# Cosine-similarity attention on one core: three of 384 score tiles exponentiated off ScalarE, and new instruction orders

## The chip, the core and the metric

The kernel runs on one core of a Trainium2 chip. The metric is device time in microseconds (us); the kernel before takes 191.36 us, the median of five runs (191.32 to 191.49). Five engines work side by side, each through its own instruction queue in order: TensorE (PE; its weight loads are shown as PEld), VectorE (DVE), ScalarE (ACT), GpSimd (POOL) and SyncE (SP, which issues DMAs). [...]

## What is computed

Q, K and V have the shape 8 x 12 x 512 x 64 in float32, and tau is 0.1. Cut to what matters, the reference is:

```python
Q_norm = Q / (np.linalg.norm(Q, axis=-1, keepdims=True) + 1e-10)
K_norm = K / (np.linalg.norm(K, axis=-1, keepdims=True) + 1e-10)
scores = np.einsum('bhqd,bhkd->bhqk', Q_norm, K_norm) / tau
weights = np.exp(scores - np.max(scores, axis=-1, keepdims=True))
weights = weights / (np.sum(weights, axis=-1, keepdims=True) + 1e-10)
return np.einsum('bhqk,bhkd->bhqd', weights, V)
```

Since a cosine lies between -1 and 1, the scores lie between -10 and 10, and the kernel takes no maximum off.

## The kernel before

The 96 heads are worked in 48 pairs, s = 0 to 47. For each pair:

- LD and LV are the loads of Q, K (`LD.s.0`, `LD.s.1`) and V; ST is the store of the output. SP issues nearly all of them, in one list.
- SQ squares Q and K (POOL, line 229). SSQ sums groups of squares with eight matmuls (line 246) and RED ends the sum (DVE, line 253; for a few pairs RED alone, line 238). NEW is a chain of eight small DVE steps for two pairs at once, an inverse square root by bit pattern and Newton steps (lines 372 to 381).
- SCL multiplies Q (DVE) and K (POOL, line 270) by the inverse norms. TR transposes them on TensorE into the PSUM bank `x_ps` (line 277; seven pairs transpose K by a DMA, XT), and EVA copies that bank to SBUF (DVE, line 468).
- SCO makes scores: `SCO.s.c` is two matmuls of 128 keys by 512 queries, one for each head of the pair (line 481), into one half of the four-bank PSUM tensor `sc_ps`. `EXP.s.c` is one ScalarE instruction that exponentiates both tiles, 128 x 1024 elements, into the bfloat16 buffer `et` (line 498). Four of these make a pair. The two halves of `sc_ps` are used in turn, so SCO waits for the EXP before the last. In the last pair, c = 0 and 1 are head 0 and c = 2 and 3 are head 1, so that a head ends early, and `EXP.47.3` is cut in two (lines 490 to 495).
- VC casts V to bfloat16 (POOL, line 503). PV multiplies the weights by V and by a column of ones that gives the row sums: `PV.s.h.t`, four matmuls each (line 514), into `o_ps`. RCP and NRM divide by the sums (DVE, lines 526 to 530). The next pair's first PV waits for NRM, which frees `o_ps`. `final` (line 535) does this for the last pair in three pieces and other banks (lines 538 to 564).

The bank `x_ps` goes round in the order in which its users stand in TensorE's list: a user that carries `take="x"` waits until the previous one's reader, named in `until`, is done. `et` has three buffers, `qk` eighteen, `qt` five, `ob` eight.

The order of work on each engine is written out in `ORDER` (line 591), one list of names per engine, made beforehand by a planner. Each engine runs its list as it stands: an instruction that waits holds up all that is behind it. `WARM` and `FILL` (lines 587 and 588) are dummy matmuls at the start (line 216): 19 before anything else and 7 placed between the first transposes.

Of the kernel before, what the change touches and what calls it, by code (L numbers as in the profile page):

```python
# [3 lines left out]
ALU = mybir.AluOpType  # L4
ACT = mybir.ActivationFunctionType
# [118 lines left out]
def bass_cosine_similarity_attention_kernel(  # L124
# [7 lines left out]
    inv_tau = 1.0 / float(tau)  # L132
# [66 lines left out]
    def scores_read(s, c):  # L199

        if s < 0:
            return None
        return ("EXP", 0, 1, c - 2) if s == 0 else ("EXP", s, c)

# [196 lines left out]
    def pair(s):  # L401
# [73 lines left out]
        for c in range(NT) if s else ():  # L475
            b = c % 2

            def sco(e, c=c, b=b):
                for i in range(2):
                    h, k = (c // 2, 2 * b + i) if last_pair else (i, c)  # L480
                    last = e.matmul(  # L481
                        out=sc_ps[:, 2 * b + i, :], lhsT=qt[iqt][64 * h : 64 * h + 64, 1, k, :],
                        rhs=qt[iqt][64 * h : 64 * h + 64, 0, :, :], start=True, stop=True)
                return last

            P.add(("SCO", s, c), "pe",
                  [("SCO", s, c - 1) if c else None, *([("EVA", s, 0), ("EVA", 1, 1, c // 2) if s == 1 else ("EVA", 2, 1)] if s in (1, 2) else [("EVA", s)]), key("XT", s),
                   scores_read(s, c - 2) if c >= 2 else scores_read(s - 1, c + 2)], sco)
            before = [("SCO", s, c), scores_read(s, c - 1) if c else scores_read(s - 1, NT - 1), key("PV", s - R_ET, 1, NT - 1)]
            if last_pair:  # L490
                for i, (h, lo, hi) in enumerate(ENDS[1:] if c == NT - 1 else [(c // 2, 0, NT)]):
                    P.add(("EXP", s, c) + ((i,) if c == NT - 1 else ()), "act", before + [key("EXP", s, c, i - 1)],
                          lambda e, b=b, h=h, q=slice(128 * lo, 128 * hi): e.activation(
                              out=et[iet][:, 2 * b : 2 * b + 2, h, q], in_=sc_ps[:, 2 * b : 2 * b + 2, q],
                              func=ACT.Exp, scale=inv_tau))
            else:
                P.add(("EXP", s, c), "act", before,
                      lambda e, c=c, b=b: e.activation(  # L498
                          out=et[iet][:, c, :, :], in_=sc_ps[:, 2 * b : 2 * b + 2, :], func=ACT.Exp, scale=inv_tau))


# [8 lines left out]
        for h in range(2):  # L510
            for t in range(NT):
                def pv(e, h=h, t=t):
                    for c in range(NT):
# [8 lines left out]
                      [scores_read(s, NT - 1), ("VC", s), before, *([("EVA", 2, 1) if h else ("EVA", 1, 1, 1), ("EVA", 0, 1, 1)] if s == 0 else [])], pv,  # L522
# [11 lines left out]

    def final(s, iq, iet, io):


        bank = [n_ps[:, :, :].rearrange("p g x -> p (g x)"), x_ps[:, :], sc_ps[:, 0, :]]
        for i, (h, lo, hi) in enumerate(ENDS):
            for c in range(NT):  # L540
                def pv(e, i=i, h=h, c=c, lo=lo, hi=hi):
                    for t in range(lo, hi):
# [7 lines left out]
                      [("EXP", s, 3, i - 1) if i and c > 1 else ("EXP", s, 2 * h + c // 2), ("VC", s),  # L550
# [14 lines left out]

    for s in range(NP):
        pair(s)
# [6 lines left out]
    if FILL[1]:  # L574
# [13 lines left out]
FILL = (7, 0)  # L588
# [4 lines left out]
        LD.0.0.0 LD.0.0.1 LD.1.0 LD.2.1 LD.2.0 LD.3.1 LD.3.0 LD.4.0 LV.0 LD.4.1 LD.5.1 LD.5.0 LD.6.1 LD.6.0 LD.7.0  # L593
        LD.7.1 LV.1 LV.3 LD.11.0 LV.2 LD.9.1 LD.9.0 LD.8.1 LD.10.0 LV.7 LD.12.1 LD.8.0 LD.12.0 LV.4 LV.9 LV.5 LD.10.1
        LV.6 LD.13.0 LD.13.1 LD.22.1 LD.11.1 LV.10 LV.8 LD.25.1 LD.20.0 LD.15.1 LD.15.0 XT.9 ST.0 LD.14.1 LD.21.0
        LD.27.1 LD.14.0 ST.2 LV.11 LD.17.1 LD.18.0 LD.17.0 LD.28.1 LD.18.1 LD.16.1 ST.5 LD.16.0 ST.1 LV.14 LV.16 LV.13
        ST.3 LD.21.1 ST.4 LD.19.1 LV.12 LD.22.0 LV.15 LV.17 LD.19.0 XT.15 LD.24.0 LD.33.0 ST.6 ST.8 LV.18 LD.20.1 ST.7
        LD.23.0 LD.23.1 LD.29.1 LD.26.0 LV.22 LD.25.0 LD.26.1 ST.10 LV.19 LD.30.0 LV.23 ST.9 LD.36.1 LD.24.1 LD.28.0
        ST.15 LD.33.1 XT.21 LV.20 ST.13 LD.27.0 LV.21 ST.11 LV.25 ST.12 LD.31.1 ST.14 LV.26 LD.39.0 LD.29.0 LV.27
        LD.31.0 ST.19 LD.36.0 LV.24 LD.34.0 LV.28 LD.30.1 ST.17 LV.33 LD.34.1 ST.16 LD.32.0 ST.18 LD.32.1 XT.27 LV.29  # L600
        LV.30 ST.21 LD.41.0 LD.35.1 LV.31 ST.22 LD.37.0 LD.35.0 ST.20 ST.25 ST.24 LD.37.1 LD.38.0 LD.38.1 LD.40.1 LV.35
        LD.47.0 LD.40.0 LD.43.1 LD.42.1 XT.33 LV.32 LD.41.1 LV.36 ST.23 LD.39.1 LV.37 LD.44.1 LV.34 LD.45.0 ST.30
        LD.45.1 LD.44.0 ST.28 LV.39 LD.43.0 ST.26 LV.42 LD.47.1 LV.38 LD.42.0 LV.40 LV.43 ST.27 LD.46.0 LD.46.1 XT.39
        LV.45 ST.29 ST.32 ST.35 LV.41 ST.33 LV.44 ST.31 ST.36 ST.39 ST.34 LV.47 ST.40 ST.38 XT.45 ST.37 ST.41 LV.46
        ST.45 ST.43 ST.42 ST.44 ST.46 ST.47.0 ST.47.1""",
    "pool": """
        SQ.0.0.1 one eye vone SQ.2.1 SQ.2.0 SQ.3.0 VC.0 SQ.4.0 SQ.5.0 SQ.6.0 VC.1 SQ.7.0 SCL.4.1 VC.2 VC.3 SCL.5.1
        SQ.9.0 SQ.8.0 SCL.6.1 VC.4 VC.5 SCL.7.1 SQ.10.0 SCL.9.1 SCL.8.1 SQ.11.0 VC.6 SQ.13.0 VC.7 SQ.12.0 VC.9 SCL.10.1
        VC.8 SCL.11.1 SQ.15.0 SQ.14.0 VC.10 SCL.12.1 SQ.17.0 SQ.16.0 SCL.13.1 SCL.14.1 VC.11 SCL.15.1 SQ.21.0 SQ.18.0
        VC.12 VC.13 SQ.19.0 SCL.16.1 VC.15 VC.14 SCL.17.1 VC.16 VC.18 SQ.20.0 SCL.18.1 SCL.19.1 VC.17 SQ.22.0 SQ.23.0  # L610
        SCL.21.1 SCL.20.1 SQ.26.0 SQ.25.0 VC.19 SQ.24.0 SCL.22.1 VC.20 SCL.23.1 VC.21 SQ.28.0 SQ.27.0 SCL.24.1 SCL.25.1
        VC.22 SQ.29.0 VC.27 VC.23 SQ.31.0 SCL.26.1 VC.24 SCL.27.1 SQ.30.0 VC.26 SQ.34.0 SCL.28.1 VC.25 SQ.32.0 SCL.29.1
        SQ.33.0 SCL.31.1 SCL.30.1 SQ.35.0 VC.29 VC.28 SQ.36.0 SCL.33.1 SCL.32.1 SQ.38.0 VC.30 SQ.37.0 VC.31 SCL.34.1
        SQ.40.0 VC.32 SCL.35.1 VC.35 VC.33 SQ.39.0 SCL.37.1 VC.36 SCL.36.1 SQ.41.0 VC.37 VC.34 VC.39 SQ.45.0 SCL.38.1
        SCL.39.1 SQ.42.0 SQ.43.0 SCL.40.1 VC.42 VC.38 SCL.41.1 SQ.44.0 SQ.46.0 VC.44 VC.40 VC.41 VC.45 SCL.42.1 SCL.43.1
        SQ.47.0 SCL.45.1 VC.43 SCL.44.1 VC.47 SCL.46.1 VC.46 SCL.47.1""",
# [3 lines left out]
        NEW.0.0 NEW.0.1 EVA.2.0 NEW.0.2 EVA.2.1 NEW.0.3 NEW.0.4 NEW.0.5 RED.4.0 NEW.0.7 NEW.0.6 SCL.3.1 SCL.3.0 RED.5.0  # L620
        RCP.0 NEW.1.0 NRM.0 EVA.3 NEW.1.1 NEW.1.2 NEW.1.3 NEW.1.4 NEW.1.5 NEW.1.7 RED.6.0 NEW.1.6 SCL.4.0 RED.7.0 RCP.1
        NRM.1 EVA.4 NEW.2.0 NEW.2.1 NEW.2.2 SCL.5.0 NEW.2.3 RCP.2 NEW.2.4 NRM.2 EVA.5 NEW.2.5 NEW.2.6 SCL.6.0 NEW.2.7
        SCL.7.0 RED.9.0 RCP.3 NRM.3 RED.8.0 NEW.3.0 NEW.3.1 EVA.6 NEW.3.2 NEW.3.3 NEW.3.4 NEW.3.5 NEW.3.7 NEW.3.6 RCP.4
        NRM.4 EVA.7 SCL.9.0 RED.10.0 SCL.8.0 EVA.9 RCP.5 NRM.5 EVA.8 RED.11.0 RED.11.1 NEW.4.0 NEW.4.1 RCP.6 NEW.4.2
        NEW.4.3 RED.13.0 NRM.6 NEW.4.4 NEW.4.5 NEW.4.7 NEW.4.6 SCL.10.0 RED.12.0 NEW.5.0 SCL.11.0 NEW.5.1 EVA.10 NEW.5.2
        RCP.7 NEW.5.3 NRM.7 NEW.5.4 NEW.5.5 EVA.11 RED.15.0 NEW.5.6 NEW.5.7 SCL.12.0 RCP.8 NRM.8 RED.14.0 NEW.6.0
        NEW.6.1 SCL.13.0 NEW.6.2 NEW.6.3 NEW.6.4 EVA.12 RCP.9 NEW.6.5 NRM.9 NEW.6.7 RED.16.1 RED.17.0 NEW.6.6 RED.16.0
        SCL.14.0 EVA.13 NEW.7.0 NEW.7.1 RCP.10 NEW.7.2 NRM.10 EVA.14 NEW.7.3 NEW.7.4 SCL.15.0 RCP.11 EVA.15 NRM.11
        RED.21.0 NEW.7.5 RED.18.0 NEW.7.7 NEW.7.6 SCL.16.0 RCP.12 NRM.12 RED.19.0 NEW.8.0 NEW.8.1 NEW.8.2 SCL.17.0
        NEW.8.3 NEW.8.4 EVA.16 NEW.8.5 NEW.8.7 RCP.13 NRM.13 NEW.8.6 EVA.17 RED.21.1 SCL.19.0 SCL.18.0 RED.20.0 RCP.14  # L630
        NEW.9.0 NRM.14 EVA.18 NEW.9.1 NEW.9.2 EVA.19 NEW.9.3 NEW.9.4 RCP.15 NRM.15 NEW.9.5 NEW.9.7 RED.22.0 NEW.9.6
        SCL.20.0 RED.23.0 RCP.16 NEW.10.0 NRM.16 EVA.20 NEW.10.1 NEW.10.2 SCL.21.0 RCP.17 NEW.10.3 NRM.17 EVA.21
        NEW.10.4 NEW.10.5 RED.26.0 RED.26.1 NEW.10.7 RCP.18 NEW.10.6 NRM.18 RED.24.0 SCL.23.0 RED.25.0 SCL.22.0 NEW.11.0
        NEW.11.1 NEW.11.2 EVA.22 NEW.11.3 RCP.19 NRM.19 NEW.11.4 NEW.11.5 NEW.11.6 NEW.11.7 EVA.23 SCL.24.0 RCP.20
        NRM.20 RED.27.0 NEW.12.0 NEW.12.1 NEW.12.2 SCL.25.0 EVA.24 NEW.12.3 NEW.12.4 RCP.21 NRM.21 NEW.12.5 EVA.25
        NEW.12.6 NEW.12.7 RCP.22 NRM.22 SCL.26.0 RED.28.0 SCL.27.0 RED.29.0 NEW.13.0 NEW.13.1 NEW.13.2 NEW.13.3 NEW.13.4
        EVA.26 RCP.23 NEW.13.5 NRM.23 EVA.27 NEW.13.7 RED.31.1 NEW.13.6 SCL.28.0 RED.30.0 RED.31.0 RCP.24 NEW.14.0
        NRM.24 EVA.28 SCL.29.0 RCP.25 NRM.25 EVA.29 NEW.14.1 NEW.14.2 NEW.14.3 NEW.14.4 NEW.14.5 NEW.14.7 RED.32.0
# [124 lines left out]
```

## Time and profile before

| what | value |
|---|---|
| median of five runs | 191.36 us |
| the profiled execution's own time | 191.32 us |
| its span, first to last instruction | 189.5 us |
| time around the span | 1.82 us |
| busy: PE, DVE, ACT, POOL | 178.3, 150.4, 181.6, 160.3 us |
| EXP of 128 x 1024, 184 of them on line 498 | 168.9 us busy |
| granted TensorE clock | full |

The page is read like this. Busy time says how long an engine had work, not whether it set the end. The chain that ended last follows the work back from the last instruction to whatever released it at each step, so it names the engine on which a shorter instruction would be felt. A row of the costliest groups gives the source line, engine, operation, written and read tensors, shapes, count, busy time, the mean duration of one, and the idle time ahead of them. Since neighbours overlap, a group's busy time over its count is the pace, and the mean duration is longer.

### The profile page before, as it was taken

The page shows a single profiled execution, that of the slowest core. Times are in us where ns is not written, and L with a number is a line of the kernel's source. Part 1 is how long each engine was busy: PE and PEld are TensorE (multiplying, and loading weights), DVE is VectorE, ACT ScalarE, POOL GpSimd, SP SyncE. Part 2 cuts the span into 40 slices and gives each one's busy share as a digit, 9 for nine tenths or more (in the row PEclk, how much of TensorE's full clock was granted, in tenths as well). Part 3 has the DMA queues.
Part 4 walks back from the last instruction along what each step waited for, and adds up shares of the span by engine and source line. Part 5 has one row for each costly group of instructions (what it writes and reads, how often), then busy time and mean ns, then how long its engine had stood idle before and what let it go on. Part 6 is the DMA issues. An engine that isn't in the chain of part 4 may idle for free.

```text
span 189.5 us, 6453 instructions
## 1 busy us (share of the span) xinstructions
PE 178.3 (94%) x2622; PEld 114.0 (60%) x2622; DVE 150.4 (79%) x453; ACT 181.6 (96%) x208; POOL 160.3 (85%) x147
## 2 busy tenths in 40 slices
PE   7999999989998999999999999999999999998982
PEld 5546666656655666656665666656665666665641
DVE  2889998797987798788977978789798696886633
ACT  5799999999999999999999999999999999999992
POOL 1899899999999999999999979989999998555000
PEclk9999999999999999999999999999999999999999
DMA  6999999999999999999999999899999980393055
GB/s 191 352 350 351 348 350 314 283 363 332 319 270 273 367 345 313 296 278 378 303 309 276 289 302 293 257 275 324 290 281 277 273 258 11 116 225 135 3 167 171
DMA packets 56238, 51.68 MB, mean 273 GB/s; under 512 B 6928, under 2 KB 56208, under 8 KB 56208
## 3 DMA queue, kind: packets, MB, share of 16 engines
q1 hardware_dynamic: 55520, 50.67, 88.8%
q10 hardware_dynamic: 688, 0.59, 1.0%
q8 instruction: 21, 0.34, 0.9%
q14 instruction: 9, 0.07, 0.1%
HBM read 37.75 MB, written 12.58 MB: 266 GB/s over the span
## 4 chain that ended last, share of the span: by engine, by line
ACT 87%; PE 10%; DVE 1%; issue 0%
ACT et L498 86%; PE scps L216 3%; PE scps L481 2%; ACT et L351 2%; PE ops L514 1%; PE xps L246 1%; PE scps L346 1%; DVE ob L558 1%; PE xps L277 0%; PE nps L543 0%; PE ops L246 0%; PE ops L312 0%; PE xps L312 0%; DVE rd L556 0%; PE ops L277 0%
## 5 line engine op out<-in xcount | busy, mean ns | idle before, releaser
L498 ACT ACTIVATE et<-scps 128x1024 bf16<-128x1024 f32 x184 | 168.9, 1182 | 0.3 <-PE scps L481 0.3
L229 POOL TENSOR_TENSOR sq<-qk 128x1024 bf16<-128x1024 f32 (+2 forms) x48 | 87.8, 1843 | 4.5 <-DMA qk<-in_Q_dram 4.0
L481 PE MATMUL scps<-qt 64*128 64x512 bf16 x376 | 73.8, 386 | 5.8 <-ACT et L498 3.7
L514 PEld LDWEIGHTS ops<-vb,et 128*128 128x128 bf16 x1504 | 53.9, 98 | 25.6 <-issue 16.7
L514 PE MATMUL ops<-vb,et 128*128 128x65 bf16 x1504 | 68.5, 194 | 0.3 <-ACT et L498 0.2
L270 POOL TENSOR_TENSOR qn<-qk,rk 128x512 bf16<-128x512 f32 x44 | 45.9, 1054 | 8.3 <-DVE rk L377 7.3
L270 DVE TENSOR_TENSOR qn<-qk,nps 128x512 bf16<-128x512 f32 x49 | 33.0, 679 | 0.6 <-ACT nps L263 0.3
L528 DVE TENSOR_TENSOR ob<-ops,rd 128x512 f32<-128x512 f32 x47 | 32.4, 690 | 0.9
L481 PEld LDWEIGHTS scps<-qt 64*128 64x128 bf16 x376 | 18.4, 93 | 23.4 <-ACT et L498 8.4
L468 DVE COPY qt<-xps 128x1024 bf16<-128x1024 bf16 (+1 forms) x45 | 29.0, 644 | 3.8 <-PE xps L277 3.5
L503 POOL TENSOR_SCALAR vb<-vf 128x512 bf16<-128x512 f32 x48 | 29.9, 637 | 1.1 <-DMA vf<-in_V_dram 1.0
L277 PE MATMUL xps<-ident,qn 128*128 128x128 bf16 x340 | 27.1, 220 | 0.2
L277 PEld LDWEIGHTS xps<-ident,qn 128*128 128x128 bf16 x340 | 19.1, 98 | 10.3 <-DVE rd L526 4.1
L246 PE MATMUL xps<-sq,ident 128*128 128x128 bf16 x304 | 23.5, 220 | 0.2
L526 DVE RECIPROCAL rd<-ops 128x8 f32<-128x8 f32 x47 | 9.7, 206 | 15.7 <-PE ops L514 14.7
L246 PEld LDWEIGHTS xps<-sq,ident 128*128 128x128 bf16 x304 | 17.2, 98 | 7.0 <-issue 3.8
L253 DVE TENSOR_REDUCE nps<-xps 128x16 f32<-128x128 f32 x37 | 11.0, 297 | 6.5 <-PE xps L246 6.2
L238 DVE TENSOR_REDUCE nps<-sq 128x8 f32<-128x512 bf16 x16 | 10.8, 684 | 0.6 <-POOL sq L229 0.6
L372 DVE TENSOR_TENSOR nps<-nps,ys 128x32 f32<-128x32 f32 (+1 forms) x46 | 9.0, 195 | 1.0
L373 DVE SCALAR_TENSOR_TENSOR nps<-nps,ys 128x32 f32<-128x32 f32 (+1 forms) x46 | 8.8, 192 | 0.8
L216 PE MATMUL scps<-warm_in 128*128 128x256 bf16 x26 | 5.6, 402 | 1.1 <-DVE warm_in L214 1.1
L216 PEld LDWEIGHTS scps<-warm_in 128*128 128x128 bf16 x26 | 3.5, 143 | 2.5 <-DVE warm_in L214 1.1
(52 smaller groups left out, 51.9 us busy)
## 6 DMA issues: line engine op xcount, KB each, us to landing
vf<-in_V_dram SPq DMA_DIRECT2D x48, 256.0 KB, 4.7
qk<-in_Q_dram SPq DMA_DIRECT2D x47, 256.0 KB, 5.0
out_dram<-ob SPq DMA_DIRECT2D x47, 256.0 KB, 4.5
qk<-in_K_dram SPq DMA_DIRECT2D x46, 256.0 KB, 4.8
qk<-in_K_dram ACTq DMA_DIRECT2D x2, 256.0 KB, 3.6
qk<-in_Q_dram SPq DMA_DIRECT2D x2, 128.0 KB, 2.7
out_dram<-ob SPq DMA_DIRECT2D x1, 128.0 KB, 2.8
qt<-qn SPq DMA_TRANSPOSE x7, 4.3
```

Source lines behind the costliest of these rows:

```text
L216: P.add(key, "pe", needs, lambda e: e.matmul(out=bank[:, 0:256], lhsT=warm_in[:, 0:128], rhs=warm_in[:, :], start=True, stop=True))
L229: emit = lambda e: e.tensor_tensor(out=b, in0=a, in1=a, op=ALU.mult)
L246: last = e.matmul(out=ps[:, 0:128], lhsT=ident[:, :], rhs=sq[s % R_SQ][:, :, 8 * k : 8 * k + 8], start=(k == 0), stop=(k == 7))
L253: lambda e: e.tensor_reduce(out=dst(None), in_=ps[:, 0:128].rearrange("p (w g e) -> p w g e", w=2, e=8), axis=AX.X, op=ALU.add))
L270: lambda e: e.tensor_tensor(out=qn[iqn][:, w].rearrange("p t h d -> p h t d"), in0=qk[iq][:, w].rearrange("p h (t d) -> p h t d", t=NT), i ...
L277: last = e.transpose(dst[:, i, :], qn[s % R_QN][:, b // NT, b % NT].rearrange("p h d -> p (h d)"), ident[:, :])
L468: lambda e: e.tensor_copy(out=qt[iqt][:, :].rearrange("p w t x -> p (w t) x")[:, 0:nb], in_=tb[:, 0:nb]))
L481: last = e.matmul(out=sc_ps[:, 2 * b + i, :], lhsT=qt[iqt][64 * h : 64 * h + 64, 1, k, :], rhs=qt[iqt][64 * h : 64 * h + 64, 0, :, :], sta ...
L498: lambda e, c=c, b=b: e.activation(out=et[iet][:, c, :, :], in_=sc_ps[:, 2 * b : 2 * b + 2, :], func=ACT.Exp, scale=inv_tau))
L503: lambda e: e.tensor_scalar(out=vb[:, iq, :, :, 0:DIM].rearrange("p c h d -> p h c d"), in0=vf[iv][:, :, :].rearrange("p h (c d) -> p h c ...
L514: last = e.matmul(out=o_ps[:, h, 65 * t : 65 * t + 65], lhsT=et[iet][:, c, h, 128 * t : 128 * t + 128], rhs=vb[:, iq, c, h, :], start=(c = ...
L528: lambda e: e.tensor_tensor(out=ob[io][:, :], in0=grid[:, :, :, 0:DIM], in1=rd[io][:, :].unsqueeze(3).to_broadcast([128, 2, NT, DIM]), op= ...
```

## The change

The first two key tiles of work that leave ScalarE are the two tiles of `SCO.46.3`, and the third is the first tile of `SCO.47.0`. `OFFS` says where each is exponentiated. Each goes through `polynomial`: one matmul `SCOX` writes the scores into the bank `x_ps`; step 0 (DVE) multiplies and adds so that the result, converted to an integer, has the float's exponent in its upper bits; step 1 (DVE) keeps the mantissa bits; five Horner steps (2 to 6) evaluate a fifth-degree polynomial of the mantissa, the last one multiplying by the float made of the bits. On VectorE a Horner step is one `scalar_tensor_tensor` that keeps its running value in `x_ps` itself; on GpSimd it is a `tensor_scalar` and a `tensor_tensor` in SBUF. Scratch is taken from `qk` buffers that are no longer loaded.

`EXP.46.3` is gone, `EXP.47.0` covers one tile, and the halves of `sc_ps` are counted by the order of the EXPs that are left (`turn`). `FILL` goes from 7 to 4. All five lists of `ORDER` are written anew; ScalarE's differs in `EXP.46.3` and in the table load, which stands before `LD.1.1` instead of after it.

```diff
-    def scores_read(s, c):
-
-        if s < 0:
-            return None
+    live = [(s, c) for s in range(NP) for c in range(NT) if None in OFFS.get((s, c), (None,))]
+    turn = {sc: i for i, sc in enumerate(live)}
+
+    def scores_read(s, c, back=0):
+
+        s, c = live[turn[s, c] - back]
         return ("EXP", 0, 1, c - 2) if s == 0 else ("EXP", s, c)
...
-        for c in range(NT) if s else ():
-            b = c % 2
...
+        chunks = [c for c in range(NT) if (s, c) in turn]
+        for c in chunks if s else ():
+            b = turn[s, c] % 2
+            kept = [i for i in range(2) if i not in off(s, c)]
...
             P.add(("PV", s, h, t), "pe",
-                  [scores_read(s, NT - 1), ("VC", s), before, *([("EVA", 2, 1) if h else ("EVA", 1, 1, 1), ("EVA", 0, 1, 1)] if s == 0 else [])], pv,
+                  [scores_read(s, chunks[-1]), *(("OFF", s, c, i, 6) for c in range(NT) for i in off(s, c)), ("VC", s), before, *([("EVA", 2, 1) if h else ("EVA", 1, 1, 1), ("EVA", 0, 1, 1)] if s == 0 else [])], pv,
                   take=None if before else "o", until=("NRM", s))
...
+    def polynomial(s, c, i):
...
+        P.add(("SCOX", s, c, i), "pe", [("EVA", s), key("XT", s)], lambda e: e.matmul(
+            out=x_ps[:, :], lhsT=qt[iqt][hs, 1, k, :], rhs=qt[iqt][hs, 0, :, :], start=True, stop=True),
+            take="x", until=(*o, 6 if inside else 0))
+        gone = [n for p in (old, more) for n in (("SQ", p, 0), ("SCL", p, 0), ("SCL", p, 1))]
+        P.add((*o, 0), "dve", [("SCOX", s, c, i)] + gone, lambda e: e.tensor_scalar(
+            out=bits.bitcast(i32), in0=x_ps[:, :], scalar1=inv_tau * 1.4426950408889634 * 2.0**23,
+            scalar2=(127.0 + SHIFT) * 2.0**23, op0=ALU.mult, op1=ALU.add))
+        P.add((*o, 1), "dve", [(*o, 0)], lambda e: e.tensor_scalar(
+            out=mant.bitcast(i32), in0=bits.bitcast(i32), scalar1=0x007FFFFF, scalar2=0xBF800000 - 2**32,
+            op0=ALU.bitwise_and, op1=ALU.bitwise_or))
+        for j, b in enumerate(HORNER):
+            last = j == len(HORNER) - 1
+            src0, by = acc if j else mant, bits if last else mant
+            dst = et[iet][:, k, h, :] if last else acc
+            free = [key("PV", s - R_ET, 1, NT - 1)] if last else []
+            if eng == "dve":
+                P.add((*o, 2 + j), eng, [(*o, 1 + j)] + free, lambda e, b=b, src0=src0, by=by, dst=dst: e.scalar_tensor_tensor(
+                    out=dst, in0=src0, scalar=b, in1=by, op0=ALU.add, op1=ALU.mult))
+                continue
+            P.add((*o, 2 + j, 0), eng, [(*o, 1 + j)], lambda e, b=b, src0=src0: e.tensor_scalar(
+                out=acc, in0=src0, scalar1=b, scalar2=1.0, op0=ALU.add, op1=ALU.mult))
+            P.add((*o, 2 + j), eng, [(*o, 2 + j, 0)] + free, lambda e, by=by, dst=dst: e.tensor_tensor(
+                out=dst, in0=acc, in1=by, op=ALU.mult))
...
-FILL = (7, 0)
+FILL = (4, 0)
+OFFS = {(46, 3): ("pool", "dve"), (47, 0): ("dve", None)}
```

The ends of the lists after the change, from where the moved steps stand:

```
pool: SQ.47.0 SCL.45.1 SCL.44.1 VC.40 VC.45 SCL.46.1 VC.41 VC.42 SCL.47.1 OFF.46.3.0.2.0 VC.43 OFF.46.3.0.2
      OFF.46.3.0.3.0 OFF.46.3.0.3 VC.44 VC.46 OFF.46.3.0.4.0 OFF.46.3.0.4 OFF.46.3.0.5.0 OFF.46.3.0.5
      OFF.46.3.0.6.0 OFF.46.3.0.6 VC.47
dve:  EVA.46 SCL.47.0 OFF.46.3.0.0 RCP.41 NRM.41 EVA.47 OFF.46.3.0.1 OFF.46.3.1.0 OFF.46.3.1.1 OFF.46.3.1.2
      RCP.42 NRM.42 OFF.46.3.1.3 OFF.46.3.1.4 OFF.46.3.1.5 RCP.43 NRM.43 OFF.46.3.1.6 OFF.47.0.0.0 RCP.44
      OFF.47.0.0.1 NRM.44 OFF.47.0.0.2 OFF.47.0.0.3 OFF.47.0.0.4 RCP.45 NRM.45 OFF.47.0.0.5 OFF.47.0.0.6
      RCP.46 NRM.46 RCP.47.0 NRM.47.0 RCP.47.1 NRM.47.1 RCP.47.2 NRM.47.2
pe:   SCO.43.0 SCOX.46.3.0 PV.41.1.0 to 3 SCO.43.1 TR.47 SCO.43.2 PV.42.0.0 to 2 SCO.43.3 SCOX.46.3.1 PV.42.0.3
      PV.42.1.0 SCO.44.0 PV.42.1.1 PV.42.1.2 SCO.44.1 PV.42.1.3 SCO.44.2 SCO.44.3 PV.43.0.0 to 3 PV.43.1.0 SCO.45.0
      PV.43.1.1 to 3 SCO.45.1 SCO.45.2 PV.44.0.0 to 3 SCOX.47.0.0 SCO.45.3 PV.44.1.0 to 3 SCO.46.0 SCO.46.1
      PV.45.0.0 PV.45.0.1 SCO.46.2 PV.45.0.2 PV.45.0.3 PV.45.1.0 to 3 SCO.47.0 SCO.47.1 SCO.47.2 PV.46.0.0 to
      PV.46.1.3 SCO.47.3 PV.47.0.0 to 3 PV.47.1.0 PV.47.2.0 PV.47.1.1 PV.47.2.1 PV.47.1.2 PV.47.1.3 PV.47.2.2 PV.47.2.3
sp:   XT.45 LV.44 LV.46 ST.36 ST.38 ST.35 LV.47 ST.37 ST.39 ST.43 ST.41 ST.44 ST.40 ST.42 ST.45 ST.46 ST.47.0 ST.47.1
```

In the lists before, `SCL.47.1` is the last entry of POOL's, and DVE's ends with `SCL.46.0 RCP.43 NRM.43 SCL.47.0 EVA.46 RCP.44 NRM.44 EVA.47 RCP.45 NRM.45 RCP.46 NRM.46` and the last pair's steps. TensorE's list before places `TR.47` between `SCO.46.0` and `SCO.46.1`, and ends with `SCO.46.3 PV.45.1.3 SCO.47.0 PV.46.0.0 to 2 SCO.47.1 SCO.47.2 PV.46.0.3 PV.46.1.0 to 3 PV.47.0.0 SCO.47.3` and the last pair's PVs.

## The prediction

> **What bounds the kernel now.** I read the page's busy times and its chain of waits first.
>
> ```profile
> PE 178.3 (94%) x2622; PEld 114.0 (60%) x2622; DVE 150.4 (79%) x453; ACT 181.6 (96%) x208; POOL 160.3 (85%) x147
> ...
> ACT 87%; PE 10%; DVE 1%; issue 0%
> ```
>
> ScalarE sets the end, with TensorE two points behind in busy time. Next the waits between engines (us in total, times, longest).
>
> ```profile
> PE scps L481 <- ACT et L498: 3.7, 14, 0.5
> ...
> ACT et L498 <- PE scps L481: 0.3, 1, 0.3
> ACT et L493 <- PE scps L481: 0.2, 1, 0.2
> ```
>
> TensorE waits for ScalarE to free score halves, hardly ever the other way round: an EXP less is an EXP sooner, as long as TensorE keeps up. TensorE's waits of 3.7 us over the whole run are all its slack. Third, the groups by form.
>
> ```profile
> L498 ACT ACTIVATE et<-scps 128x1024 bf16<-128x1024 f32 x184 | 168.9, 1182 | 0.3 <-PE scps L481 0.3
> L270 POOL TENSOR_TENSOR qn<-qk,rk 128x512 bf16<-128x512 f32 x44 | 45.9, 1054 | 8.3 <-DVE rk L377 7.3 <-DVE nps L377 1.0
> L528 DVE TENSOR_TENSOR ob<-ops,rd 128x512 f32<-128x512 f32 x47 | 32.4, 690 | 0.9
> L503 POOL TENSOR_SCALAR vb<-vf 128x512 bf16<-128x512 f32 x48 | 29.9, 637 | 1.1 <-DMA vf<-in_V_dram 1.0
> L493 ACT ACTIVATE et<-scps 128x512 bf16<-128x512 f32 x2 | 1.1, 604 | 0.0
> ```
>
> EXPs follow each other every 168.9/184 = 0.918 us. Last, stretches of the end (busy us of PE, PEld, DVE, ACT, POOL) and its timeline.
>
> ```profile
> 165.00:170.00 5.00, 4.70 (x77) 3.04 (x76) 4.85 (x15) 5.00 (x7) 3.23 (x4) 1.00 0.97 217
> 170.00:175.00 5.00, 4.37 (x69) 2.62 (x69) 2.62 (x9) 5.00 (x6) 2.67 (x3) 1.00 0.46 157
> 175.00:180.00 5.00, 4.98 (x87) 3.27 (x84) 3.23 (x6) 5.00 (x7) 0.00 (x0) 1.00 0.01 3
> ```
> ```profile
> 180.91 0.59 PE L481 MATMUL scps<-qt 64*128 64x512 bf16 x2 [0.39 <-DVE rd L526]
> ...
> 181.54 1.06 ACT L493 ACTIVATE et<-scps 128x1024 bf16<-128x1024 f32 x1
> ...
> 182.85 2.92 ACT L493 ACTIVATE et<-scps 128x1024 bf16<-128x1024 f32 x4 [0.25 <-PE scps L481]
> ...
> 185.82 0.30 PE L543 MATMUL scps<-vb,et 128*128 128x65 bf16 x4 [0.20 <-ACT et L493]
> ```
>
> POOL is free from 175 us and DVE has about half its time after 170 us, so helpers exist just where ScalarE still works to 185.77 (182.85 + 2.92). PE, though, is full from 175 to 180.
>
> [...]
>
> **Part 1, the EXPs removed.** `EXP.46.3` gives 0.918. `EXP.47.0` with one tile costs what a cut EXP adds at the end: the four EXPs in 2.92 us are two of 0.918 and two of the cut size, which, with 0.1 of overhang, leaves 0.49 each. It saves 0.43. Gross: 1.35 us.
>
> **Part 2, what TensorE gives back at the end.** Times are those of before, EXP.46.2 ending about 180.77. EXP.47.0 then ends at 181.26. SCO.47.1 needs the half that EXP.46.2 leaves; its two matmuls use the same rows and take 0.59 (the row at 180.91), so it ends at 181.41, and EXP.47.1 (1.02 long alone) ends at 182.48: 0.3 lost, because half an EXP no longer covers a SCO. SCO.47.2 follows to 181.95. Then all of PV.46, 32 matmuls at 0.66 per 16, stands ahead of SCO.47.3: to 183.25, SCO.47.3 to 183.83, and the two cut EXPs end at 184.93, where an unbroken row would end at 181.26 + 2 x 0.918 + 2 x 0.49 = 184.08. The stalls are 0.85 together; before, the same passage lost 0.35 (0.25 ahead of EXP.47.1 and its overhang). So ScalarE ends 185.77 - 184.93 = 0.84 earlier, not 1.35. The last PV, RCP, NRM and store behind it (3.7 us to the span's end) stay as they are; the stores ahead in SP's queue are the same bytes.
>
> **Part 3, the polynomials.** A DVE tile is one PSUM read (0.69 by line 528), one SBUF step[...] and five Horner steps at 0.69 with some 0.035 between dependent ones: 4.7 to 5.0 us. The GpSimd tile costs DVE 1.1 to 1.4 and POOL 5 x (0.637 + 1.054) = 8.5. DVE so gets 10.5 to 11.4 us more after about 166, POOL 8.5. TensorE gets three SCOX of 0.27 for a pair of 0.33 and a single, +0.2. To make room, the steps of pair 47 up to EVA.47 come some 9 us sooner (TR.47 from 177.6 to about 167.8, after SCO.43.1). Walking DVE's list with these costs from EVA.47 at 168.5: tile 46.3.1 starts at 169.9, NRM.42 ends 172.6, NRM.43 175.5, step 6 176.2. SCOX.47.0.0 wants the bank at 176.3 and stands ahead of SCO.45.3, which may end at latest 0.15 before EXP.45.2 does. It fits with nothing over. Next, NRM.45 ends 181.85, PV.46 wants it at 181.95. The GpSimd tile, started at 169.5, with VC.43, VC.44 and VC.46 between, ends near 180; PV.46 wants it at 181.95: 2 us to spare. VC.43 is queued behind a GpSimd step that waits for DVE, done 170.7, wanted 172.9.
>
> **The unknown[...].** Four DVE steps meet a busy POOL: steps 1 and 2 of both DVE tiles (step 2 reads the mantissa twice from SBUF; later steps have the PSUM bank as one input). Each waits nothing at best and a whole POOL step, 1.05, at worst, so 0 to 4.2; with both DVE intervals free of slack, nearly all reaches the end. [...] I take 0.3, half of a 0.637 us POOL step, once: POOL's chain is itself dependent and leaves gaps[...]. I am least sure of this value.
>
> **Part 4, the start.** FILL loses three dummies, one ahead of the first transpose. That transpose started at 6.09, behind dummies at 0.213 us each (x23 in 5.06 us), while its data were ready by 5.8. EVA, SCO.0.0.0 (7.35) and the first EXP (7.77) move 0.2 earlier; at most 0.2, since then DVE (SCL at 6.01 for 0.41) is next. The table load ahead of LD.1.1 may delay that load by up to the table's 1.28; SQ.1.1 at 5.82 has it at 5.45 now, ScalarE idles 0.82 before its first EXP, so up to 0.9 is covered; if cover fails, 0.35 is lost. I take -0.2, ends -0.2 and +0.35. POOL's first memset goes into a 3.8 us wait for a load: nothing.
>
> **Part 5, other orders.** TensorE does by SCO.43.2 some 2.2 us more than before at that point (a sum of row durations along both lists, taken from the first score on: two eight-block transposes, a four-block one, a SCOX and some PVs). Before, it idled 0.6 + 0.8 + 0.6 + 0.06 us between 100 and 160 and 0.4 to 168: about enough. SCOs that reach ScalarE late by under 0.3 are hidden by the half in hand. I take 0, ends 0 and +1.0. XT.45 goes ahead of LV.44 in SP's list, with SCL.45.1 earlier too. That list delays stores 35 to 44; `ob` has eight buffers and NRM.43 needs ST.35, issued near 161 behind LV.46: covered by some 10 us. LV.47 is behind ST.38, wanted by VC.47 only at 180.
>
> **Sum.** Against the profiled 191.32 (span 189.5 + 1.82; the median is 191.36): -0.2 - 0.84 + 0.3 = 190.58, so 190.6.
>
> **Rivals.**
> *Ports eat it.* The four waits come to about 1.0 on DVE's list, a mean of 0.25 each. 191.32 - 1.04 + 1.0 = 191.3: no change. For: POOL is busy without a break from 169.5 to about 180. Against: luck of alignment.
> *VectorE becomes the bound of the end: slower.* With waits of 0.5 each (half of 1.05) NRM.42, NRM.43 and NRM.45 come 2.0 late; PV.43 and PV.45 stand at the head of TensorE's list until `o_ps` is free, SCOs behind them starve ScalarE, and SCO.47.3 goes 2 us late: 191.32 - 1.04 + 2.0 = 192.3. It decides from 1.04 of waits on. For: no slack in part 3's walk, and DVE was at 4.85 of 5.00 us in 165 to 170. Against: none of it is measured.
> *Pair 47 not ready.* NEW, SCL and TR of pairs 46 and 47 must be 9 us sooner; if POOL's SCL.47.1 misses 167.7 by 1.5 us, TR.47 blocks TensorE: 191.8. For: POOL waits 8.3 us for norms on line 270, which this pulls forward. Against: four VCs (2.5 us) go behind SCL.47.1, so that POOL's busy 160.3 - 2.5 from its first load at 4.3 on, with the 4.0 us that it idles between 10 and 160, ends at 166.1.
> *It doesn't do what it says:* not possible; the lists fix that EXP.46.3 is gone.
>
> **Chances.** Forecast (190.1 to 190.95) 0.47; ports even it out (191.0 to 191.7) 0.23; VectorE the bound (191.75 to 192.8) 0.22; pair 47 late or a disturbed start 0.08, three quarters of it slower. About 0.2% (0.38 us) is what a measurement of this kernel can tell from no change. Faster: 0.47 + 0.02 = 0.49. Same: 0.23. Slower: 0.22 + 0.06 = 0.28. Low end 190.1: no port waits (190.28) and stores that land 0.2 sooner. High end 192.2 reaches into the slower case. The forecast's own range is 190.1 to 190.95.
>
> **What would show it.** Right: 183 EXPs on the old pace, first EXP near 7.57, ScalarE's only new stalls at EXP.47.1 and EXP.47.3, last EXP ending 185.0 or sooner. Port waits show as steps 1 and 2 that last or start over 0.3 later than their input allows while POOL is busy. Wrong: waits of TensorE on RCP/NRM or x_ps between 170 and 183, ScalarE idle before 180, POOL's SCL.47.1 after 167.7, Horner steps of over 0.75 us.

## The result, and the profile after

The changed kernel takes 192.18 us (median of 42 runs, 191.67 to 194.35) against 191.56 for the kernel before in the same comparison (79 runs, 190.98 to 192.74). The ratio is 1.0041, 95% interval 1.0028 to 1.0053: slower by 0.4% (the two medians alone give 1.0032), where 190.6 and faster was forecast. The profiled run of the changed kernel took 192.17 us, with a span of 190.0 us (before: 189.5). Of the rivals it is the second that came, VectorE as the bound of the end, priced at 192.3.

The page of the changed kernel, busy times and chain that ended last:

```profile
PE 177.3 (93%) x2619; PEld 113.3 (60%) x2619; DVE 160.0 (84%) x469; ACT 180.7 (95%) x207; POOL 170.6 (90%) x157
...
ACT 78%; PE 12%; DVE 5%; DMA 2%; issue 1%
```

ScalarE has less to do, as meant. But it held 87% of the chain before and holds 78% now, and VectorE went from 1% to 5%: somewhere the end is now waiting for VectorE. The waits say where (us in total, times, longest):

```profile
PE scps L494 <- ACT et L512: 2.9, 9, 0.5
PE ops L532 <- DVE ob L546: 2.3, 3, 1.4
ACT et L512 <- PE scps L494: 1.4, 3, 0.7
...
ACT et L506 <- PE scps L494: 0.4, 1, 0.4
```

The second row is new. TensorE waits 2.3 us in three places for the NRM that empties `o_ps`, and ScalarE, which lost 0.3 and 0.2 us to TensorE before, loses 1.4 and 0.4. TensorE's timeline has the three places, PV.43, PV.44 and PV.45:

```profile
173.57 0.77 PE L532 MATMUL ops<-vb,et 128*128 128x65 bf16 x20 [0.68 <-DVE ob L546]
...
176.47 0.65 PE L532 MATMUL ops<-vb,et 128*128 128x65 bf16 x16 [0.30 <-DVE ob L546]
...
180.52 0.42 PE L532 MATMUL ops<-vb,et 128*128 128x65 bf16 x8 [1.35 <-DVE ob L546]
```

Why the NRMs are late is on VectorE's timeline. L575 is step 1 of a tile, L584 with `xps<-qk` is step 2:

```profile
168.81 0.42 DVE L575 TENSOR_SCALAR qk<-qk 128x512 int32<-128x512 int32 x1
...
170.26 0.66 DVE L575 TENSOR_SCALAR qk<-qk 128x512 int32<-128x512 int32 x1
170.95 1.64 DVE L584 SCALAR_TENSOR_TENSOR xps<-qk 128x512 f32<-128x512 f32 x1
...
178.41 1.45 DVE L575 TENSOR_SCALAR qk<-qk 128x512 int32<-128x512 int32 x1
...
180.39 0.68 DVE L584 SCALAR_TENSOR_TENSOR xps<-qk 128x512 f32<-128x512 f32 x1
```

The first row is the step 1 that met a GpSimd without work: 0.42. The same instruction takes 0.66 at 170.26 and 1.45 at 178.41. Step 2 takes 1.64 at 170.95 and 0.68 at 180.39. GpSimd's timeline beside it (L521 is VC, L589 the `tensor_tensor` that is the second half of its Horner step):

```profile
170.01 0.63 POOL L521 TENSOR_SCALAR vb<-vf 128x512 bf16<-128x512 f32 x1
170.60 1.44 POOL L589 TENSOR_TENSOR qk<-qk 128x512 f32<-128x512 f32 x1
...
178.32 1.26 POOL L589 TENSOR_TENSOR qk<-qk 128x512 f32<-128x512 f32 x1
...
180.42 1.77 POOL L589 TENSOR_TENSOR et<-qk 128x512 bf16<-128x512 f32 x1
```

Lay the two lists over each other. VC.43 ends at 170.64, and the step 1 that was ready at 170.26 ends at 170.92. The `tensor_tensor` that GpSimd begins at 170.60 ends at 172.04, and step 2 ends at 172.59. The one from 178.32 ends at 179.58, and step 1 of the last tile at 179.86. Each time VectorE's instruction lasts until GpSimd's is over and then for most of its own length more: 0.28, 0.55 and 0.28 us. At 180.42 it goes the other way: step 2 was there first with 0.68, and GpSimd's instruction, 1.27 elsewhere, takes 1.77. Against the undisturbed durations (step 1 0.42, step 2 0.69) VectorE waited 0.24 + 0.95 + 1.03 = 2.22 us. The trace of e9_padded_waits, the same kernel with other TensorE work added, repeats the four lengths to 0.02 us (0.66, 1.64, 1.47, 0.68). The chain of the changed kernel, in order of time, runs through just these rows:

```profile
170.26 0.67 DVE qk L575
170.95 0.41 DVE xps L584
171.36 1.14 issue
...
178.41 1.45 DVE qk L575
...
180.52 0.42 PE ops L532 x8
```

The row `issue` is the rest of step 2, for which the chain names no cause; behind an undisturbed Horner step, at 174.80, it has 0.20 there. The row at 178.41 stands between RCP.44 and NRM.44 in VectorE's list, so that NRM.44, and with it PV.45, is late by the whole wait.

In all these meetings the engine whose row begins first keeps going, and the other's row ends only after it: VectorE's three rows above, and GpSimd's 1.77. What is left to do after the wait is less than the whole instruction: 0.28 of 0.42 and 0.55 of 0.69 on VectorE, 1.12 of 1.27 on GpSimd (to 182.19, with step 2 over at 181.07). Steps 1 and 2 need only VectorE's own step before them (`polynomial`), so the two engines hold each other up where no semaphore links them. The recorded texts call these port waits; the name is the author's supposition of a cause, and the traces show who waits and for how long, not through what. The prediction has no row of before with such a wait either: that these four steps would meet GpSimd was its author's estimate. What it had left open was only how often.

The granted TensorE clock differs between runs of the changed kernel: a mean of 0.997 or more in a quarter of them (median 191.94 us), 0.986 to 0.991 in over half (192.11), 0.976 to 0.982 in a fifth (193.9); whether that is part of the loss is asked in the last two experiments.

### The profile page after: what moved, and what is told of

Read it like the earlier page. It is cut to its first block, busy times and chain, and to the rows that moved or that the text cites. A ratio compares the mean times of both kernels' runs of the same rounds, so it can differ in the third digit from the quotient of the medians.

```text
span 190.0 us, 6480 instructions
## 1 busy us (share of the span) xinstructions
PE 177.3 (93%) x2619; PEld 113.3 (60%) x2619; DVE 160.0 (84%) x469; ACT 180.7 (95%) x207; POOL 170.6 (90%) x157
## 4 chain that ended last, share of the span: by engine, by line
ACT 78%; PE 12%; DVE 5%; DMA 2%; issue 1%
ACT et L512 75%; PE ops L532 4%; PE scps L494 4%; DMA qk<-in_K_dram 2%; ACT et L361 2%; PE xps L287 1%; DVE xps L584 1%; DVE qk L575 1%; DVE ob L546 1%; PE xps L256 1%; PE scps L356 1%; DVE xs L307 1%; DVE ob L615 1%; PE xps L568 0%; PE ops L322 0%
## 5 line engine op out<-in xcount | busy, mean ns | idle before, releaser
L521 POOL TENSOR_SCALAR vb<-vf 128x512 bf16<-128x512 f32 x48 | 30.2, 642 | 0.2
L587 POOL TENSOR_SCALAR qk<-qk 128x512 f32<-128x512 f32 x5 | 3.5, 694 | 3.3 <-DVE qk L575 3.0
L226 PE MATMUL scps<-warm_in 128*128 128x256 bf16 x23 | 4.9, 397 | 1.1 <-DVE warm_in L224 1.1
```

The lines of the kernel that those rows point to most:

```text
L521: lambda e: e.tensor_scalar(out=vb[:, iq, :, :, 0:DIM].rearrange("p c h d -> p h c d"), in0=vf[iv][:, :, :].rearrange("p h (c d) -> p h c ...
```

## The experiments

Each kernel ran beside the kernel before on the same chip; ratios are to that (191.63 us for the first eight, 191.46 for the last two, which ran on another chip). In e1 and e8 a part of the weights is another function, and in e2 a part is left out, as their expectations say, so only their times count.

### VectorE's two steps read the PSUM bank instead of SBUF (e1_dve_psum)

```diff
-            out=mant.bitcast(i32), in0=bits.bitcast(i32), ...
+            out=mant.bitcast(i32), in0=(x_ps[:, :] if inside else bits).bitcast(i32), ...
...
-            src0, by = acc if j else mant, bits if last else mant
+            src0, by = acc if j or inside else mant, bits if last else mant
```

> In the two VectorE tiles, step 1 reads the score bank in PSUM instead of the bits in SBUF, and step 2 takes its first operand from that bank instead of reading the mantissa twice; so no VectorE step has two SBUF inputs or runs within SBUF. The weights of these two tiles are then not the exponentials (that part of the computation is replaced); GpSimd's tile is whole. Ports theory (VectorE waits for GpSimd's SBUF steps: 0.24 + 0.95 + 1.03 = 2.2 us in the changed kernel's trace): steps 1 and 2 take 0.69 each, 0.55 more work in all but no wait, VectorE's list is 1.65 us earlier, TensorE no longer waits 0.68 and 1.35 us on NRM; about 190.8 us, 0.6 below the kernel before. Load theory (VectorE's added work itself, whatever the ports do): 0.55 us more work, no gain, 192.2 or more. Orders theory (the loss is in the new orders): 192.2.

Measured: 190.22 us, ratio 0.9926 (0.9902 to 0.9950). GpSimd's tile runs whole beside it. VectorE's timeline of this kernel:

```profile
170.24 0.69 DVE L575 TENSOR_SCALAR qk<-xps 128x512 int32<-128x512 int32 x1
170.96 0.70 DVE L584 SCALAR_TENSOR_TENSOR xps<-xps,qk 128x512 f32<-128x512 f32 x1
...
177.51 0.64 DVE L575 TENSOR_SCALAR qk<-xps 128x512 int32<-128x512 int32 x1
```

Step 1 is dearer by itself (0.69, not 0.42), yet no step waits. NRM.42, NRM.43 and NRM.45 end at 172.49, 175.40 and 181.66, where the prediction's walk had 172.6, 175.5 and 181.85. With VectorE's instruction count and GpSimd's load unchanged, 1.1% is won by which memory two operands lie in. So neither VectorE's load nor the new orders made the changed kernel slow. The time is 0.6 below the 190.8 that the ports theory expected; the next two kernels come out below it too, by 0.35 to 0.4.

### GpSimd's ten steps on 64 of 512 columns (e2_pool64)

```diff
+            acc_, src0_, by_, dst_ = (x[:, 0:64] for x in (acc, src0, by, dst))
```

> GpSimd's ten polynomial steps work on 64 of the 512 columns of their tile (the other 448 columns' weights of that tile are left out, and stay what the buffer held); every order, every VectorE and TensorE instruction stays. Ports theory: GpSimd's steps fall from 0.62 and 1.27 us to about 0.2, so VectorE's three waits of 2.2 us in all fall to about 0.3 (one can still meet a cast of V of 0.63); about 190.6 us. Load theory: VectorE's work is the same; 192.2. Orders theory: 192.2.

Measured: 190.22 us, ratio 0.9923 (0.9901 to 0.9946). Here VectorE is untouched and GpSimd is short. VectorE's timeline:

```profile
170.16 0.56 DVE L575 TENSOR_SCALAR qk<-qk 128x512 int32<-128x512 int32 x1
...
177.44 0.38 DVE L575 TENSOR_SCALAR qk<-qk 128x512 int32<-128x512 int32 x1
```

Only one wait is left, 0.56 instead of 0.42 in step 1 (step 2 takes 0.70 and 0.69). It is for the cut `tensor_tensor` on GpSimd, since VC.43 is over at 170.17:

```profile
170.12 0.32 POOL L590 TENSOR_TENSOR qk<-qk 128x64 f32<-128x64 f32 x1
```

That one ends at 170.44, and step 1 lasts 0.28 more, as in the changed kernel. The time is that of e1_dve_psum. Two different edits, one on each side of the conflict, give the same 1.1%.

### No tile on GpSimd (e3_no_pool_tile)

```diff
-OFFS = {(46, 3): ("pool", "dve"), (47, 0): ("dve", None)}
+OFFS = {(46, 3): (None, "dve"), (47, 0): ("dve", None)}
```

In the lists the steps of that tile go, and SCO.46.3 (ahead of PV.45.1.2) and EXP.46.3 (for one tile) come back.

> The first tile of SCO.46.3 goes back to ScalarE (an EXP of one tile, 0.49 us), the other two tiles stay on VectorE. Ports theory: GpSimd has only casts of V after 166 us, VectorE waits at most once for one (0.3), and has 1.1 us less work; ScalarE has 0.49 more than at best: about 190.3 + 0.5 = 190.8 us. Load theory: VectorE's list is 1.1 us shorter of some 11 added, so at best 1.1 of the loss comes back: 191.2 to 191.7. Orders theory: 192.2 + 0.2.

Measured: 190.45 us, ratio 0.9938 (0.9916 to 0.9960). The whole of the computation is done, so this version is faster than the kernel before by 0.6% and than the changed one by about 1%. ScalarE does one tile more, and it is still faster: the GpSimd tile cost more than it took off.

### The orders alone (e4_orders_alone)

```diff
-OFFS = {(46, 3): ("pool", "dve"), (47, 0): ("dve", None)}
+OFFS = {}
```

> No tile leaves ScalarE; the new orders, FILL of 4 and the table load ahead of LD.1.1 stay, EXP.46.3 and SCO.46.3 are put back in their places. Ports and load theory: the orders cost nothing by themselves; the start is 0.1 us earlier, the end has a stall of about 0.5 ahead of EXP.47.3 because all of PV.46 stands before SCO.47.3 (0.35 before): 191.3 to 191.6, within 0.2 of the kernel before. Orders theory: 192.2 plus what the polynomials saved, so 192.5 or more.

Measured: 191.76 us, ratio 1.0000 (0.9983 to 1.0017). The orders by themselves cost nothing that can be seen; their gain is not seen here either, for which see e10_orders_padded.

### One tile's waits taken away (e8_psum_one_tile)

The edit of e1_dve_psum, for tile (46, 3) alone:

```diff
+        n, psum = len(scratch), (s, c, i) == (46, 3, 1)
...
+            src0, by = acc if j or psum else mant, bits if last else mant
```

> Of the two VectorE tiles only that of the chunk (46, 3) has its bit step read, and its second step take its first operand, from the x_ps bank (so that tile's weights are another function); tile (47, 0) is as in the changed kernel. Theory (the waits of VectorE for GpSimd are what was lost): the waits of 0.24 and 0.95 us at tile (46, 3) go, NRM.42 and NRM.43 end near 172.5 and 175.4 as in e1_dve_psum, the wait of about 1.03 at tile (47, 0) stays. VectorE's end chain is then about 1.0 to 1.2 us later than in e1_dve_psum where NRM.45 ends, of which the walk had about 1 us of cover: 190.2 to 190.9 us. Rival (each wait costs its full length in the end): 191.0 to 191.2 us.

Measured: 190.66 us, ratio 0.9955 (0.9938 to 0.9971). The waits did not stay as they were: with everything a little earlier, the last tile met GpSimd at another point. VectorE's timeline:

```profile
177.37 0.48 DVE L575 TENSOR_SCALAR qk<-qk 128x512 int32<-128x512 int32 x1
...
178.37 1.16 DVE L584 SCALAR_TENSOR_TENSOR xps<-qk 128x512 f32<-128x512 f32 x1
```

Against the 0.38 and 0.69 that these two steps take undisturbed in e2_pool64, these are waits of 0.10 + 0.47 = 0.57 us, not 1.03. Above e1_dve_psum the time is (0.9955 - 0.9926) x 191.6 = 0.56 us, or 0.44 by the medians. That agreement proves little: each ratio is uncertain by about 0.002, so 0.4 us, and in e1_dve_psum both step 1s are about 0.27 dearer by themselves, here only one. The pair that differs in GpSimd's work alone, with the same list on VectorE, is the changed kernel and e2_pool64. There the waits are 2.22 and 0.14 us, NRM.45 ends 15.17 and 13.22 us after EVA.47 began, 1.95 later, and the medians are 192.18 and 190.22, 1.96 apart. So a wait reaches the end nearly whole. The 1 us of cover that my theory for this run gave VectorE is not there; the median is inside the range that I gave, but for another reason, a shorter wait.

### The same steps by way of PSUM, for the full computation (e5_copy, e6_copy_sco)

```diff
+        m = x_ps[:, :] if inside else mant
-            out=mant.bitcast(i32), in0=bits.bitcast(i32), ...
+            out=m.bitcast(i32), in0=bits.bitcast(i32), ...
+        if inside:
+            P.add((*o, 1), "dve", [(*o, 1, 0)], lambda e: e.tensor_copy(out=mant, in_=m))
```

> The complete computation. In the two VectorE tiles the bit step writes the mantissa into the x_ps bank instead of SBUF, a copy of it from there to SBUF is added, and the first Horner step takes one operand from each; no VectorE step then has two SBUF streams in both operands or an SBUF source with an SBUF result. Theory: no waits for GpSimd (2.2 us go) against two added copies of 0.4 to 0.7 us each: 0.8 to 1.4 us more of VectorE's work than in e1_dve_psum, within or just over its cover of about 1 us: 190.2 to 190.8 us. Rival (waits are not the cause, VectorE's sum of work is): 192.6 to 193.5 us, the changed kernel's time with the copies on top.

Measured: 192.56 us, ratio 1.0050 (1.0033 to 1.0068). A miss, at the lower edge of the rival's range. No step waits for GpSimd (steps 1 and 2 and the copy take 0.67 to 0.70), so that half of the theory held, but the cover was missing again. The two copies are 1.38 us on VectorE, and NRM.45 ends 15.1 us after EVA.47 began, as late as in the changed kernel: TensorE waits 2.1 us for the NRMs (2.3 there). What costs time at the end is that VectorE's list is late; in the changed kernel waits made it so, here work does. The seven runs with a clock of 0.998 or more have a median of 191.8, which is 1.6 above e1_dve_psum, about the price of the copies. Two more things happened in the profiled run, which took 194.43 us. ScalarE's timeline at the start:

```profile
7.18 1.15 ACT L237 ACTIVATE sq<-qk 128x512 bf16<-128x512 f32 x2 [1.30 <-DMA qk<-in_K_dram]
```

The load LD.1.1, which the change puts behind the table load, came so late that SQ.1.1 waited 1.30 us and the first EXP began at 8.23, not near 7.6. And near the end the clock fell, in stretches of 3 us (busy PE, PEld, DVE, ACT, POOL, then the granted clock):

```profile
179.00:182.00 3.00, 1.55 (x24) 0.98 (x25) 2.93 (x5) 2.31 (x4) 2.74 (x4) 0.95 0.18 57
182.00:185.00 3.00, 3.00 (x22) 1.13 (x19) 2.83 (x6) 1.92 (x3) 0.39 (x1) 0.50 0.75 253
185.00:188.00 3.00, 3.00 (x37) 1.99 (x37) 1.10 (x3) 1.26 (x2) 0.00 (x0) 0.50 0.22 71
```

TensorE was busy for half of the stretch from 179 to 182, and then ran at half the clock for over 6 us, through all that decides the end. The 194.43 us hold for that run, not for the median.

e6_copy_sco is e5_copy with one move more in TensorE's list:

```diff
-        ... PV.46.1.0 PV.46.1.1 PV.46.1.2 PV.46.1.3 SCO.47.3
+        ... PV.46.1.0 SCO.47.3 PV.46.1.1 PV.46.1.2 PV.46.1.3
```

> The complete computation: e5_copy, and TensorE's SCO.47.3 moved ahead of the last three groups of PV.46. If the stall left before EXP.47.3 in e1_dve_psum (0.45 to 0.76 us late behind PV.46) is due to that order, it goes, 0.3 to 0.6 us below e5_copy. If TensorE's sum of work at the end decides instead, no change from e5_copy.

Measured: 193.17 us, ratio 1.0073 (1.0049 to 1.0098), no gain. Its six runs have clocks from 0.989 to 0.999. At like clocks the move costs: 192.4 in the two runs at 0.998 and 0.999, against 191.8 in e5_copy, and 193.35 in the three at 0.989 and 0.990, against 192.6 there. The profiled run reached EVA.47 at the same time as that of e5_copy (168.75), and its TensorE was busy for as long between 179 and 182, but the clock did not fall:

```profile
179.00:182.00 3.00, 1.55 (x28) 0.98 (x29) 2.93 (x5) 2.31 (x4) 2.74 (x4) 1.00 0.18 57
```

### No tile on GpSimd, and SCO.47.3 earlier (e7_no_pool_sco)

The same move in TensorE's list as in e6_copy_sco, made in e3_no_pool_tile.

> The complete computation: the version without the GpSimd tile (e3_no_pool_tile), and TensorE's SCO.47.3 moved ahead of the last three groups of PV.46. If the order holds EXP.47.3 up: 0.3 to 0.6 us below e3_no_pool_tile, 189.9 to 190.2 us. If TensorE's sum decides: 190.4 to 190.5 us.

Measured: 191.24 us, ratio 0.9978 (0.9966 to 0.9989): slower than e3_no_pool_tile by 0.8, where a gain or nothing was expected. ScalarE's stall is gone. Its last rows in this kernel:

```profile
181.60 3.63 ACT L506 ACTIVATE et<-scps 128x512 bf16<-128x512 f32 x5
186.94 0.39 ACTq L619 DMA_DIRECT2D out_dram<-ob  x1
```

In e3_no_pool_tile the last EXP ended at 185.05 and the store was issued at 186.04: 1.0 later. Here the EXPs end at 185.23, without a break, and the store goes out 1.7 later. What is late next is VectorE:

```profile
184.86 0.69 DVE L546 TENSOR_TENSOR ob<-ops,rd 128x512 f32<-128x512 f32 x1
...
186.62 0.29 DVE L615 TENSOR_TENSOR ob<-scps,rd 128x128 f32<-128x128 f32 x1
```

PV.46 ends later for the move, NRM.46 therefore begins at 184.86 (183.68 in e3_no_pool_tile), and the last three RCPs and NRMs queue behind it without a gap. The stall at EXP.47.3 had been hiding PV.46. Of the 1.4 us between the two profiled spans (189.7 and 188.3) this explains a part: EVA.47 began 0.52 later already (the first EXP 0.38, for Q's data at 3.59, not 3.17), the store's issue lost 0.38 more, and the rest, 0.5, lies behind it. That the move itself costs does not rest on this pair alone: e6_copy_sco lost 0.6 to 0.7 by it. How the 0.8 of the medians divides is open.

### TensorE kept busy where it waits (e9_padded_waits, e10_orders_padded)

```diff
+    for k in range(14):
+        dummy(("pad", k), n_ps[:, :, :].rearrange("p g x -> p (g x)"), [("SCL", 47, 0), ("SCL", 47, 1)])
```

> The changed kernel (complete computation) with 14 matmuls of 128x256 added on TensorE, whose results nobody reads, in the places where TensorE waits for NRM: four ahead of PV.43.0.0, two ahead of PV.44.0.0, eight ahead of PV.45.0.0. In runs of the changed kernel the mean granted clock was 1.0 in some (191.8 us), 0.991 in many (192.1) and 0.982 in a few (193.9). Theory (TensorE's idle time in those waits is what the throttle answers to): the clock stays at 0.994 or more in every run and the median comes to 191.7 to 191.9 us; the waits for NRM keep their ends, so no more than that is gained. Rival (the clock has nothing to do with these waits): the same mixture of clocks, 192.1 to 192.3 us.

Measured: 192.23 us, ratio 1.0033 (1.0022 to 1.0044). The clock did what the theory says: 0.995 to 1.0 in all fourteen runs. The time did not: it stays that of the changed kernel. TensorE's timeline of this kernel shows why:

```profile
179.22 1.05 PE L226 MATMUL nps<-warm_in 128*128 128x256 bf16 x8
180.66 0.42 PE L532 MATMUL ops<-vb,et 128*128 128x65 bf16 x8 [0.39 <-DVE ob L546]
```

The added matmuls fill the wait, and PV.45 starts when the NRM lets it, as before. So a clock kept up did not win the median back. The changed kernel's own runs set the clock's share at 0.2 us or so (192.18 for all of them, 191.94 for those at 0.997 or more), against some 2 us for the waits on GpSimd. In the fifth of the runs at 0.976 to 0.982 it is about 2 us.

> The orders alone (no tile taken from ScalarE, complete computation) with 20 such matmuls in the places where TensorE waits for ScalarE between 171 and 183 us. In e4_orders_alone the clock was 0.995 to 1.0 in half the runs (191.3 to 191.5 us) and 0.988 to 0.991 in the other half (192.1). Theory: the clock stays at 0.994 or more and the median is 191.3 to 191.5 us, 0.1 to 0.2 below the kernel before, which is what the orders are worth without the throttle. Rival: a mixture of clocks as before, 191.7 to 191.9 us.

Measured: 191.30 us, ratio 0.9987 (0.9976 to 0.9997), clocks of 0.995 to 1.0 in all 22 runs, as the theory has it. In e4_orders_alone seven of fourteen runs had a clock of 0.991 or less and a median of 192.11, the other seven 191.32. The new orders, with the new start, are thus worth about 0.1% (0.2 us), which the lower clock in half the runs hid there. These two kernels ran on another chip, without the same kernels unpadded beside them, so that this chip grants more clock is not excluded as the reason. The trace of e5_copy shows what a low mean consists of: 0.981 over its 192.4 us is by my estimate 7.3 us at half the clock (2 x 0.019 x 192.4), and 6 of them are the two stretches at 0.50 above. What brings the clock down is not shown: TensorE was busy for 1.55 of 3 us ahead of the drop in e5_copy, and for just as much in e6_copy_sco and 1.65 in the changed kernel, whose profiled runs kept the clock at 1.00 up to 188 us.

## Why the prediction was wrong

**The step that failed** is "The unknown", VectorE's waits for GpSimd, in its last choice. The sum lies within the bounds 0 to 4.2, and the four places were right. The value taken, 0.3, "half of a 0.637 us POOL step, once", measured 2.22: 0.24 and 0.95 at the first VectorE tile, 1.03 and 0 at the second. The reason given for a low value, that GpSimd's dependent chain leaves gaps, is refuted: the gaps between its dependent steps are some 0.1 us (178.24 to 178.32, for one), and step 2, ready at 170.95 right behind its step 1 (to 170.92), still lasted until after GpSimd's `tensor_tensor`, whose row begins at 170.60 and ends at 172.04. The instruction that meets VectorE there is also longer than the bound allowed, 1.27 undisturbed with an fp32 result, and not 1.054. The text itself had the better estimate, "0.5 each", in the rival that came true: 2.0 us and 192.3, against 2.22 and 192.18. Its mean came true, not its even spread: two meetings cost nearly a whole step, one a quarter of a microsecond, one nothing. So close a match is in part luck. At four meetings with an engine that is busy nearly all the time, about half a step for each is what an arbitrary start would give on average (this is argued, not shown); a value near the low end needed a reason that this list of instructions forbids a meeting, and there was none.

**That it all reaches the end** held. Both DVE intervals were said to be free of slack; against e2_pool64 the changed kernel has 2.08 us more of waits and takes 1.96 more.

**Parts 1 and 2** (the EXPs removed, what TensorE gives back) held within 0.3: e1_dve_psum, the changed kernel without the waits, has the last EXP end at 184.74, where the 184.93 less 0.2 for the start gives 184.73. But its first EXP began at 7.71, 0.14 later than forecast, and the end passage lost less than was said: 0.34 ahead of EXP.47.3 (0.55 in the walk), since PV.46's 32 matmuls took 1.15 and not 1.3, and about 0.14 at EXP.47.1 (0.3 in the walk; the three EXPs there take 2.57, unbroken 2.43). In the changed kernel the stalls begin at EXP.45.0 and the last EXP ends at 186.44.

**Part 3** (the walk down VectorE's list) held within 0.2 us wherever nothing waited, as e1_dve_psum shows. The low end of its tile, 4.7, needs a step 1 of some 0.4 us, for which the prediction shows no row of before: it was the author's estimate, and the trace after gives 0.42. GpSimd's tile was priced at 8.5 and ended "near 180". It ended at 182.19: five halves at 0.62 and five at 1.27 are 9.5 by themselves, and its own waits came on top. This was not what held PV.46 up.

**Part 4** (the start, -0.2) held once the load is set aside: the first EXP began at 7.68 in the profile after, 0.09 earlier, but counted from ScalarE's second SQ, which waits for K's load in both (3.91 before, 4.04 after), 0.22 earlier. It ranged from 7.55 to 8.23 over the profiles of the experiments, and in all but one it came 3.64 to 3.70 after that SQ, where it was 3.86 before. The risk named there, a late LD.1.1, cost time in that one, e5_copy.

**Part 5** (the other orders, 0) held, as did the pair 47 that was ready in time: TR.47 stood at 167.5 and blocked nothing. Parts 4 and 5 together were put at -0.2; e10_orders_padded gives -0.2 (0.06 to 0.46 by its interval).

The sum without waits was 190.58 - 0.3 = 190.3, a gain of 1.0 on before. e1_dve_psum gives 0.9926 x 191.32 = 189.9, a gain of 1.4. So the term for the waits was 1.9 too small. The remaining terms look 0.4 too cautious, but the interval of that ratio is 0.5 us to either side, so they may as well have been right.

## What to carry to other kernels

Before work is given to GpSimd beside VectorE, list VectorE's instructions in that stretch of the two kinds that waited here, an int32 `tensor_scalar` from SBUF to SBUF and a `scalar_tensor_tensor` with both operands in SBUF. Charge each with half of GpSimd's step (2.22 us for four of them here) unless the orders keep them apart; in e1_dve_psum, with one operand of each in PSUM, they took 0.64 to 0.70 us and none waited, though the first of the two kinds is by itself longer so (0.69, not 0.42). A helper that is idle is not free if its use stops another engine on the path: leaving the GpSimd tile on ScalarE (e3_no_pool_tile) gave 190.45 us, the best full version measured. And at the end of a kernel look for what the present stall is hiding, as PV.46 and NRM.46 in e7_no_pool_sco, before that stall is removed.

## What the hardware showed that was not expected

- The waits go both ways and lengthen GpSimd's rows too: `tensor_tensor` of 128x512 in fp32 takes 1.27 us undisturbed, 1.44 and 1.77 where VectorE had begun first; `tensor_scalar` 0.62, and 0.94.
- A wait lengthens the row of the instruction instead of showing as idle time ahead of it: the groups by form give 842 ns for step 1 in the changed kernel and 400 without the GpSimd tile, while the last column, idle time ahead of it, is 0.0 in both. Of the changed kernel:

```profile
L575 DVE TENSOR_SCALAR qk<-qk 128x512 int32<-128x512 int32 x3 | 2.5, 842 | 0.0
```

- With TensorE busy for 1.55 of 3 us near the end, the granted clock fell to 0.50 for over 6 us in one profiled run and stayed at 1.00 in another; with 14 or 20 matmuls for nobody in the gaps it was 0.995 or more in all 36 runs, on another chip.
